# First attention scores asked for three gate tiles later, and the scans' loads in another order

## The chip, the cores and the metric

The kernel runs on one core of a Trainium2 chip. The metric is the device time of one execution in microseconds (us), lower is better. Three runs of the kernel before gave 1560.87, 1555.83 and 1557.04 us: median 1557.04. The engines are named as in the profile: PE (TensorE matmul) with PEld (its weight loads), DVE (VectorE), ACT (ScalarE), POOL (GpSimd), SP (SyncE, which here only issues DMAs).

## What is computed

One layer of a diffusion backbone over 1024 latent tokens and 256 context tokens, width 1024, fp32. Half of the width is a gated DeltaNet with 4 heads of 128, scanned forward and backward, the other half a neighbourhood attention with 8 heads of 64. Cut to the parts that the change touches:

```python
# group A: one scan per direction, chunk by chunk
v_new = u_i - w_i @ S
o_i = (q_i * exp(gam_i)) @ S + qk_i @ v_new
S = S * exp(g_last) + k_dec.T @ v_new
o = rms_norm(o_f + rev(o_b), out_norm_w) * silu(z)      # z: the output gate
# group B: softmax over window keys and all context keys
s = concatenate([q @ k_win + bias, q @ k_ctx])
o = softmax(s) @ v
x = x + g1 * (concatenate([dn_x, na_x]) @ w_out)
x = x + g2 * swiglu(modulate(rms_norm(x)))
```

## The kernel before

The program runs in stages, all unrolled: the modulation and norm; a list of input projections ("jobs"); the two scans with the attention beside them; the output projection; the feed-forward net. A matmul in fp32 precision is made from split operands (a high and a low part), so most products are three matmuls.

**The last projections.** The jobs are column blocks of the combined input projection. The last three are value blocks of the DeltaNet and, as the very last job, `Wide("z", 0)`: half of the gate z. It has eight tiles of 128 tokens (line 595, 24 matmuls of 128x256 each). Beside its tiles run the transposes of the last two value blocks (line 527), which DVE scales (line 531) and SP stores to the DRAM tensor `v_d` (line 535).

**The attention** is a generator, `attention` (called `fill` where it is stepped). Its first step loads heads, context values and the first biases. It has 32 pairs (two heads x one 128-query block). A pair takes two steps' worth of scores (line 303, written S below, one half for each head), a maximum on DVE (305), an exponential on ACT (307), scaling on DVE (308, 309), transposes on PE (314, T below), a copy by ACT (317), and the product with the values (324, PV below). The score banks `sc` have two buffers, the bias tiles `bt` four, so each new pair's biases wait until an older pair is transposed; `bt` is cleared in part by POOL (271) and loaded by SP (272).

**The scans** work through ten chunks of 128 tokens in each direction. `load` issues a chunk's tiles on SP: keys by features `kT`, values `v`, keys by tokens `kt`, queries by features `qT`, the block inverse `y`, and `at`. `scan` uses them in this order: for all but the first chunk `kT` with the state (line 1195); `qT` with the state (1205) from chunk 2 on; `y` with the values (1214); `at` (1226); `kt` for the new state (1231). The first chunk of a direction has no state, so its first matmul is that of `y` and `v`. For every step of a scan or of `finish`, `beside(PACE)` adds PACE to a counter, and each whole unit in it steps the attention once.

**What sets the order.** Program order is only a wish: a list scheduler places each instruction on its engine's queue by priority and by its own reckoning of when operands are ready. On the chip every engine then runs its queue strictly in order, and so does SP with its DMAs: an SP row that has to wait holds all rows behind it.

Of the kernel before, what the change touches and what calls it, by code (L numbers as in the profile page):

```python
# [51 lines left out]
NCONST = 4 * 128 + 4 * 32  # L52
WIN = (256, 0)
CTX = {256: slice(0, 256), 0: slice(384, 640)}
PACE = 0.63
AHEAD = {(1, 0): (3,), (1, 1): (3, 4), (2, 0): (4, 5), (2, 1): (5, 6, 7), (3, 0): (6, 7)}
ORDER = [list(range(NCH)), [1, 0] + list(range(9, 1, -1))]

# [30 lines left out]
def hybrid(ctx, tc, a, dbg):  # L89
# [3 lines left out]
    def pools(stack, name, side=None, bufs=1, **kw):  # L93
        if side:
            kw["side"] = side
        return stack.enter_context(tc.tile_pool(name=name, bufs=bufs, reuse_waits="tile", **kw))
# [43 lines left out]
    v_d = dram.tile([T, 512], F32, name="v_d", tag="v_d")  # L140
    k_d = dram.tile([T, 512], F32, name="k_d", tag="k_d")
    z_d = dram.tile([L, 512], F32, name="z_d", tag="z_d")
    kT_d = dram.tile([128, NCH, 4, 128], F32, name="kT_d", tag="kT_d")
    qT_d = dram.tile([128, 8, 4, 128], F32, name="qT_d", tag="qT_d")
# [6 lines left out]
    y_d = dram.tile([2, NCH, 128, 4, 128], F32, name="y_d", tag="y_d")  # L151
# [102 lines left out]
    def attention(nw):  # L254
# [74 lines left out]

        order = [(hp, half, cb) for hp in range(NAH // 2) for half in range(2) for cb in range(4)]  # L330
        heads = {0: [load(0), load(1)]}
        vcs = {0: context(0)}
        bt, vw = biases(*order[0]), values(*order[0])
        yield 1
        old = None
        for n, (hp, half, cb) in enumerate(order):
            if half == 1 and cb in (0, 2) and hp + 1 < NAH // 2:
                heads.setdefault(hp + 1, []).append(load(2 * hp + 2 + cb // 2))
                if cb == 0:
                    vcs[hp + 1] = context(hp + 1)  # L340
            if cb == 0:
                out = nw.tile([128, 512], F32, name="no", tag="no")
            if old:
                next(old)
            cur = pair(heads[hp], bt, vw, vcs[hp], half, cb, out)
            next(cur)
            if n + 1 < len(order):
                bt, vw = biases(*order[n + 1]), values(*order[n + 1])
            yield 1
            if old:  # L350
                next(old)
                if cb == 0:
                    store(*done)
            if cb == 3:
                done = out, hp, half
            old = cur
            yield 1
# [17 lines left out]
    with ExitStack() as bs:  # L375
# [537 lines left out]
        fl = lambda x: x.rearrange("p a b -> p (a b)")  # L913
# [126 lines left out]
        def blk(n):  # L1040
            return jobs[n] if 0 <= n < len(jobs) and isinstance(jobs[n], Block) else None
# [9 lines left out]
        for n in range(2, len(jobs) + 2):  # L1051
            j = jobs[n] if n < len(jobs) else None
            if n == inv:
                early.close()
                psum.append(psa.enter_context(tc.tile_pool(name="psa", bufs=1, space=PSUM)))
                bg.add(block_inverses())
                bg.add(preps())
            final = n == len(jobs) - 1
            if n == len(jobs) - 2:
                bg.drain()  # L1060
                bg2.drain()
                late.close()
                sp1 = pools(middle, "sp1", "left")
                zpool[0] = sp1
                jobs[n + 1].room()
                fill = attention(pools(attn, "nw", "left", 2))
                next(fill)
            if final:
                psa.close()
                psum.append(scan_psum.enter_context(tc.tile_pool(name="psg", bufs=1, space=PSUM)))  # L1070
            if n + 1 < len(jobs):
                jobs[n + 1].prefetch()
            fin = blk(n - 2) if n - 2 not in done else None
            fin = fin.finish() if fin else iter(())
            nrm = blk(n - 1)
            if isinstance(j, Wide):
                for t, _ in enumerate(j.tiles()):
                    if t > 1 or not final:
                        next(fin, 0)
                    if final:  # L1080
                        next(fill)
                    if t == 4 and nrm:
                        nrm.norm()
                        for _ in fin:
                            pass
                        fin = nrm.finish()
                        done.add(n - 1)
                        nrm = None
                    bg.step(2)
            elif j:  # L1090
                for k in range(KT):
                    j.mm([k])
                    if k >= 3:
                        next(fin, 0)
                    bg.step(1)
                    if n > inv + 4:
                        bg2.step(1)
                j.evac()
            for _ in fin:
                pass  # L1100
            done.add(n - 2)
            if isinstance(j, Wide) and n == values:
                vlat = nv_d[CT:].rearrange("(r c) d -> r c d", c=64)
                for cb in range(4):
                    for ch in range(4):
                        for r in range(4):
                            sp.dma_start(vw_d[r * 32:r * 32 + 32, :, cb, ch],
                                         vlat[4 * ch + r, BLKS[cb]:BLKS[cb] + 32].rearrange("c (h d) -> c h d", d=128))
            if nrm:
                nrm.norm()  # L1110
            if isinstance(j, Block):
                j.silu()
# [7 lines left out]
    fl = lambda x: x.rearrange("p a b -> p (a b)")  # L1120
# [20 lines left out]
    with ExitStack() as gs:  # L1141
# [10 lines left out]
        def work(name, bufs=2, dt=F32):  # L1152
            return sw.tile([128, 4, 128], dt, name=name, tag=name, bufs=bufs)
# [6 lines left out]
        def load(d, c, near):  # L1160

            def tile_of(name, src):
                t = work(name, 3) if name == "v" else sl.tile([128, 4, 128], F32, name=name, tag=name)
                sp.dma_start(fl(t), src)
                return t

            both = shared.pop(c, None)
            if both is None:
                r = slice(c * 128, (c + 1) * 128)
                both = [tile_of("kT", fl(kT_d[:, c])), tile_of("v", v_d[r])]  # L1170
                both += [tile_of("kt", k_d[r]), tile_of("qT", fl(qT_d[:, c - 2])) if c >= 2 else None]
                if c in near:
                    shared[c] = both
            y = tile_of("y", fl(y_d[d, c]))
            at = tile_of("at", fl(at_d[d, c - 2])) if c >= 2 else None
            kT, v, kt, qT = both
            ready[d, c] = kT, qT, kt, v, y, at

        seen = set()
# [102 lines left out]
        def beside(n):  # L1282
            count[0] += n
            while count[0] >= 1:
                count[0] -= 1
                next(fill, 0)

        for d in range(2):
            load(d, ORDER[d][0], (ORDER[1 - d][1],))
        for i in range(NCH):  # L1290
# [5 lines left out]
            while live:  # L1296
                nxt = []
                for n, g in enumerate(live):
                    if next(g, 0):
                        nxt.append(g)  # L1300
                    beside(PACE)
                live = nxt
# [51 lines left out]
    class Stream:  # L1354
# [67 lines left out]
        def next(self, n=2):  # L1422

            while len(self.got) < n:
                self.make()
            out = [self.got.pop(0) for _ in range(n)]
            return out
# [347 lines left out]
```

## Time and profile before

| what | value |
|---|---|
| median of three runs | 1557.04 us (1555.83 to 1560.87) |
| profiled execution, its own time | 1556.61 us |
| its span, first to last instruction | 1554.8 us |
| mean granted TensorE clock | 0.979 |
| last gate tiles, about | 556 to 608 us |
| scans and attention, about | 608 to 820 us |
| output projection and feed-forward net | 820 us to the end |
| DMA traffic | 267.35 MB, mean 172 GB/s |

The span is cut into stages by the lines that run in them. In a row of the windows view stand the stretch, its length, then for each engine the busy time in us with the number of instructions, then the granted TensorE clock, the share of the DMA engines that is busy, and GB/s. In the view of waits a row says which engine and line waited for which engine and line (or DMA): the total in us, how often, and the longest. In the timeline the first two numbers are the start and the duration in us, and a bracket at the end tells the idle time before and what ended it. PE's matmuls are pipelined, so the durations of neighbours overlap; what a group costs is read from its start to the next one's start.

### The profile page before, as it was taken

Reading aid. Unit: us, or ns where it says so; the run is one execution under the profiler, and the core shown is the slowest. Engines: PE = TensorE matmul, PEld = TensorE weight load, DVE = VectorE, ACT = ScalarE, POOL = GpSimd, SP = SyncE. Lnnn points to the kernel's source line nnn. Section 1 sums busy time; section 2 is a strip of 40 time slices with the busy share of each in tenths; the row PEclk is TensorE's granted clock in tenths of the full one; section 3 lists DMA queues with packets and bytes.
Section 4 is the critical chain, followed back from the end, with each engine's and each line's share of the span. In section 5 each row is a group of like instructions: output and inputs, shape, how many; then the busy total and the mean of one; then the engine's idle time right before and its main releaser. Section 6 shows DMA issues by size and latency. Waiting matters only on the chain. (4 is left out here: it accounts for less than half of the span.)

```text
span 1554.8 us, 23965 instructions
## 1 busy us (share of the span) xinstructions
PE 1486.3 (96%) x8702; PEld 1239.4 (80%) x8702; DVE 993.5 (64%) x1712; ACT 727.8 (47%) x1404; POOL 234.1 (15%) x286
## 2 busy tenths in 40 slices
PE   6999999999899978999999999999999999999998
PEld 4788787677678858888887878888888888888887
DVE  5774496674454544667986559865666656689652
ACT  5442552535754336665874266333333334454440
POOL 1154500733625110111210000000000000000000
PEclk9999998899989979999999999999999999999999
DMA  9274221578545466888737601632222224698742
GB/s 388 62 222 126 72 75 55 163 228 241 191 145 183 137 186 193 298 275 265 241 101 246 228 34 59 225 107 105 102 102 102 103 101 156 228 376 290 243 143 82
DMA packets 204118, 267.35 MB, mean 172 GB/s; under 512 B 16736, under 2 KB 114528, under 8 KB 202976
## 3 DMA queue, kind: packets, MB, share of 16 engines
q1 hardware_dynamic: 198480, 261.07, 50.7%
q10 hardware_dynamic: 5520, 4.76, 0.9%
q8 instruction: 68, 1.11, 0.3%
q14 instruction: 50, 0.41, 0.1%
HBM read 201.02 MB, written 68.94 MB: 174 GB/s over the span
## 5 line engine op out<-in xcount | busy, mean ns | idle before, releaser
L405 PE MATMUL blk<-hh,whi 128*128 128x512 f32 (+1 forms) x410 | 124.3, 396 | 2.4 <-ACT kk L550 1.4
L1412 ACT CAST uhi<-wq 128x512 fp32r<-128x512 f32 x101 | 61.0, 622 | 131.9 <-issue 84.9
L1412 ACT CAST uhi<-ws 128x512 fp32r<-128x512 f32 x91 | 54.0, 621 | 146.4 <-PE ps L1351 96.5
L405 PE MATMUL blk<-hl,whi 128*128 128x512 f32 (+1 forms) x410 | 117.5, 379 | 0.3 <-DVE hl L707 0.3
L595 PE MATMUL blk<-zw,hh 128*128 128x256 f32 (+1 forms) x576 | 115.2, 294 | 0.9 <-ACT kk L550 0.8
L405 PE MATMUL blk<-hh,wlo 128*128 128x512 f32 (+1 forms) x410 | 115.1, 378 | 0.6 <-POOL wlo L200 0.6
L1413 DVE TENSOR_TENSOR ulo<-wq,uhi 128x512 fp32r<-128x512 f32 x101 | 67.6, 687 | 58.8 <-ACT uhi L1412 32.4
L1351 PE MATMUL ps<-hT,uhi 128*128 128x512 f32 x336 | 103.6, 390 | 0.0
L1351 PE MATMUL ps<-lT,uhi 128*128 128x512 f32 x336 | 103.5, 389 | 0.0
L1351 PE MATMUL ps<-hT,ulo 128*128 128x512 f32 x336 | 103.5, 389 | 0.0
L595 PEld LDWEIGHTS blk<-zw,hh 128*128 128x128 f32 x576 | 93.0, 193 | 4.7 <-issue 2.0
L1351 PE MATMUL ps<-hB,uhi 128*128 128x512 f32 x288 | 89.2, 391 | 0.6 <-ACT hB L1526 0.6
L1351 PE MATMUL ps<-lB,uhi 128*128 128x512 f32 x288 | 88.8, 389 | 0.4 <-DVE lB L1527 0.4
L1351 PE MATMUL ps<-hB,ulo 128*128 128x512 f32 x288 | 88.7, 389 | 0.0
L405 PEld LDWEIGHTS blk<-hh,wlo 128*128 128x128 f32 x410 | 72.7, 193 | 15.4 <-POOL wlo L200 0.9
L405 PEld LDWEIGHTS blk<-hh,whi 128*128 128x128 f32 x410 | 69.9, 194 | 18.6 <-issue 4.5
L405 PEld LDWEIGHTS blk<-hl,whi 128*128 128x128 f32 x410 | 72.9, 193 | 14.5 <-DVE hl L707 0.8
L595 PE MATMUL blk<-zw,hl 128*128 128x256 f32 (+1 forms) x288 | 83.5, 290 | 0.0
L1351 PEld LDWEIGHTS ps<-hT,ulo 128*128 128x128 f32 x336 | 63.1, 188 | 13.2
L1351 PEld LDWEIGHTS ps<-lT,uhi 128*128 128x128 f32 x336 | 63.1, 188 | 13.1
L1351 PEld LDWEIGHTS ps<-hT,uhi 128*128 128x128 f32 x336 | 62.9, 188 | 12.9
L200 POOL TENSOR_TENSOR wlo<-wraw,whi 128x1024 fp32r<-128x1024 f32 x18 | 45.3, 2517 | 180.6 <-ACT whi L199 173.2
(359 smaller groups left out, 3544.5 us busy)
## 6 DMA issues: line engine op xcount, KB each, us to landing
wq<-w_fo SPq DMA_DIRECT2D x99, 256.0 KB, 4.3
wq<-w_gu SPq DMA_DIRECT2D x88, 256.0 KB, 2.8
wad<-wa SPq DMA_DIRECT2D x64, 256.0 KB, 4.6
bt<-rpb SPq DMA_DIRECT2D x64, 192.0 KB, 3.5
t_d<-g SPq DMA_DIRECT2D x22, 512.0 KB, 3.6
fr<-t_d SPq DMA_DIRECT2D x44, 256.0 KB, 5.1
f_d<-g SPq DMA_DIRECT2D x33, 256.0 KB, 2.1
fr<-f_d SPq DMA_DIRECT2D x33, 256.0 KB, 4.1
```

The costliest lines, as they stand in the source:

```text
L200: lo_engine.tensor_tensor(o, r, h.bitcast(F32), OP.subtract)
L405: pe.matmul(o, ww[:, k], xx[k][:, s], start=k == 0 and j == 0, stop=k == KT - 1 and j == 2)
L595: pe.matmul(p[:, :c1 - c0], x[k][:, s], ww[:, k, c0:c1], start=k == 0 and j == 0, stop=k == KT - 1 and j == 2)
L1351: pe.matmul(o, w[wi][:, k], x[xi][:, k], start=first and k == 0 and j == 0, stop=k == n - 1 and j == 2, skip_group_check=True)
L1412: act.copy(hi, self.raw[key])
L1413: dve.tensor_tensor(lo, self.raw[key], hi.bitcast(F32), OP.subtract)
```

## The change

Three edits. In the last gate job the attention is stepped only from the fourth tile on, so five times and not eight. PACE goes from 0.63 to 0.66. In the scans' `load` the order of the issues in the program is `v`, `kt`, `y`, `kT`, `qT`, `at`, where it was `kT`, `v`, `kt`, `qT`, `y`, `at`. No operation is added or removed.

```diff
-PACE = 0.63
+PACE = 0.66
...
                 for t, _ in enumerate(j.tiles()):
                     if t > 1 or not final:
                         next(fin, 0)
-                    if final:
+                    if final and t > 2:
                         next(fill)
...
             if both is None:
                 r = slice(c * 128, (c + 1) * 128)
-                both = [tile_of("kT", fl(kT_d[:, c])), tile_of("v", v_d[r])]
-                both += [tile_of("kt", k_d[r]), tile_of("qT", fl(qT_d[:, c - 2])) if c >= 2 else None]
+                both = [tile_of("v", v_d[r]), tile_of("kt", k_d[r])]
+                y = tile_of("y", fl(y_d[d, c]))
+                both += [tile_of("kT", fl(kT_d[:, c])), tile_of("qT", fl(qT_d[:, c - 2])) if c >= 2 else None]
                 if c in near:
                     shared[c] = both
-            y = tile_of("y", fl(y_d[d, c]))
+            else:
+                y = tile_of("y", fl(y_d[d, c]))
             at = tile_of("at", fl(at_d[d, c - 2])) if c >= 2 else None
-            kT, v, kt, qT = both
+            v, kt, kT, qT = both
             ready[d, c] = kT, qT, kt, v, y, at
```

The lines behind the edit in `load` move down by two (1214 becomes 1216, 1231 becomes 1233). What the scheduler makes of it is seen on the engines' queues, at three places. Rows are instructions in queue order; names carry a number for each buffer.

**PE, where the last projection block (405) meets the attention and the gate.** `sc_5126` and `sc_5233` are the scores of pairs 0 and 1, `blk` a gate tile. The changed kernel has:

```order
L405 MATMUL blk_4894<-hh7_458,wlo_4711 128x512
L303 MATMUL sc_5126<-kh_4859,qs_4858 128x256
L303 MATMUL sc_5233<-kh_4859,qs_4858 128x256
L303 MATMUL sc_5126<-kh_4867,qs_4866 128x384
L314 MATMUL sc_5126<-cst_72,bt_4876 128x128 x2
L595 MATMUL blk_5005<-zw_4854,hh0_129 128x256
```

Here nothing moved. Row for row the kernel before has the same lines and forms in the same places, down to the end of the third gate tile: the scheduler puts the scores of the first pairs ahead of the gate in both. Only the numbers of two score buffers differ.

**PE, from the last gate tile to the scans' first matmul.** One row stands for each group (its first row). Before, with `sc_5252`, `sc_5371`, `sc_5555`, `sc_5630` the scores of pairs 2, 3, 4, 5:

```order
L595 MATMUL blk_5399<-zw_4854,hh7_458 128x256
L527 MATMUL m_5427<-cst_72,cacc_4985 128x128 x2
L324 MATMUL sc_5252<-pt_5362,vc_4874 64x128
L314 MATMUL sc_5371<-cst_72,bt_5272 128x128 x5
L303 MATMUL sc_5555<-kh_4859,qs_4858 128x256
L314 MATMUL sc_5371<-cst_72,bt_5275 128x128 x5
L324 MATMUL sc_5371<-pt_5546,vc_4874 64x128
L314 MATMUL sc_5555<-cst_72,bt_5391 128x128 x5
L303 MATMUL sc_5630<-kh_4859,qs_4858 128x256
L1214 MATMUL ps_5509<-v_5490,y_5494 128x128 x4
```

Now, with `sc_5233`, `sc_5350`, `sc_5511` the scores of pairs 1, 2, 3:

```order
L595 MATMUL blk_5304<-zw_4854,hh7_458 128x256
L527 MATMUL m_5332<-cst_72,cacc_4985 128x128 x2
L314 MATMUL sc_5233<-cst_72,bt_5146 128x128 x5
L303 MATMUL sc_5350<-kh_4859,qs_4858 128x256
L314 MATMUL sc_5233<-cst_72,bt_5149 128x128 x5
L324 MATMUL sc_5233<-pt_5341,vc_4874 64x128
L314 MATMUL sc_5350<-cst_72,bt_5253 128x128 x5
L303 MATMUL sc_5511<-kh_4859,qs_4858 128x256
L314 MATMUL sc_5350<-cst_72,bt_5256 128x128 x4
L1216 MATMUL ps_5445<-v_5424,y_5428 128x128 x4
```

The scans' first matmul follows the gate after nearly the same amount of attention, but that attention is two pairs younger: the groups between the gate tiles went behind the gate.

**SP, from the loads of the first output weights (195) to the scans' first `y`.** In brackets stand the semaphores a row waits for; a DMAHW one is an earlier DMA's landing. Before:

```order
L195 DMA wraw<-w_out 128x8x128 [waits DMAHW2_49,PE_49]
L195 DMA wraw<-w_out 128x8x128 [waits DMAHW3_49]
L535 DMA v_d<-vt 128x10x128 [waits DMAHW4_49,DVE_49]
L272 DMA bt<-rpb 128x384 [waits DMAHW5_49,DMAHW6_49,PE_49,Pool_49]
L278 DMA vw<-vw_d 128x384 [waits DMAHW7_49]
L272 DMA bt<-rpb 128x384 [waits DMAHW0_49,PE_49,Pool_49]
L1164 DMA kT<-kT_d 128x512 [waits DMAHW1_49]
L1164 DMA v<-v_d 128x512 [waits DMAHW4_49,DMAHW2_49]
L1164 DMA kt<-k_d 128x512 [waits DMAHW3_49,Activation_49]
L1164 DMA y<-y_d 128x512
```

Now:

```order
L195 DMA wraw<-w_out 128x8x128 [waits DMAHW5_49,PE_49]
L195 DMA wraw<-w_out 128x8x128 [waits DMAHW6_49]
L272 DMA bt<-rpb 128x384 [waits DMAHW7_49,PE_49,Pool_49]
L535 DMA v_d<-vt 128x10x128 [waits DMAHW0_49,DVE_49]
L272 DMA bt<-rpb 128x384 [waits DMAHW2_49,PE_49,Pool_49]
L1164 DMA v<-v_d 128x512 [waits DMAHW3_49,DMAHW0_49]
L1164 DMA kt<-k_d 128x512 [waits DMAHW4_49]
L1164 DMA y<-y_d 128x512 [waits DMAHW5_49,Activation_49]
```

`v` now leads the scans' loads, `y` is third and not fourth, and a bias load stands ahead of the last value store. In both, the first `v` waits for that store's landing. From the output projection (line 1328 before) to the end PE's queue is the same in both kernels.

## Prediction

> **What bounds the kernel now.** I read the page first, then the windows by stage, PE's waits, and the timelines of PE and SP where the windows showed idle time. The page's first part and two of its slice rows:
>
> ```profile
> PE 1486.3 (96%) x8702; PEld 1239.4 (80%) x8702; DVE 993.5 (64%) x1712; ACT 727.8 (47%) x1404; POOL 234.1 (15%) x286
> ...
> PE   6999999999899978999999999999999999999998
> PEclk9999998899989979999999999999999999999999
> ```
>
> PE is busy for 96% of the span, the next engine, DVE, for 64%. Only slices 14 to 16 of 40 (39 us each, 544 to 622 us) show PE with a visible hole, and the clock row dips there too. By stage (stretch, length, busy us of PE, PEld, DVE, ACT, POOL, then clock, DMA share, GB/s):
>
> ```profile
> 556.40:570.90 14.50, 3.98 (x18) 2.20 (x19) 10.50 (x17) 5.59 (x8) 0.77 (x3) 0.57 1.07 291
> 570.90:607.60 36.70, 36.56 (x306) 34.54 (x304) 13.51 (x31) 16.49 (x33) 3.97 (x7) 0.94 0.43 124
> 607.60:626.00 18.40, 13.72 (x108) 11.05 (x106) 9.08 (x20) 14.81 (x29) 2.51 (x5) 0.81 0.99 327
> 626.00:820.00 194.00, 190.18 (x1793) 167.05 (x1792) 150.70 (x456) 134.18 (x383) 30.19 (x61) 1.00 0.73 233
> ...
> 835.00:1554.80 719.80, 714.58 (x3162) 590.47 (x3160) 469.16 (x738) 287.89 (x486) 0.00 (x0) 1.00 0.46 158
> ```
>
> The first row is the opening, between the last value block and the gate: PE does 4.0 us of work in 14.5, at a clock of 0.57. The second is the gate, full. The third is the seam between the gate and the scans: 13.7 of 18.4 busy, clock 0.81. In the fourth, scans and attention, PE is idle for 3.8 us of 194; in the rest of the kernel it is full. So a change here gains by closing the opening or the seam, and in the fourth stage it can gain 3.8 us at most. PE's waits in the opening:
>
> ```profile
> PE sc L303 <- DMA kh<-nk_d: 4.9, 1, 4.9
> PE sc L303 <- DVE mx L305: 3.6, 1, 3.6
> PE sc L314 <- DVE bt L309: 1.9, 1, 1.9
> ```
>
> Together 10.4 us: the first scores wait for the keys' landing, then for the maximum on DVE, then the first transposes for the scaled exponentials.
>
> **The opening: nothing.** The edit asks for the first scores three tiles later, but PE's queue has them where they were, ahead of the gate, row for row to the third gate tile. SP's, ACT's, DVE's and POOL's queues are the same up to there too. The 10.4 us stay. The edit does not do here what it says.
>
> **The seam.** What moves is the attention between the gate tiles. From the order rows, these groups went from before to behind the gate's end: T and PV of pair 1, S and T of pair 2, S of pair 3. Their price stands where scan and attention alternate without a wait (start to next start):
>
> ```profile
> 631.87 0.76 PE L314 MATMUL sc<-cst,bt 128*128 128x128 f32 x5
> 632.47 0.61 PE L1214 MATMUL ps<-vn,y 128*128 128x128 f32 x4
> 632.92 0.27 PE L303 MATMUL sc<-kh,qs 128*128 128x256 f16 x1
> ...
> 633.46 1.28 PE L1214 MATMUL ps<-vn,y 128*128 128x128 f32 x10
> 634.67 0.32 PE L324 MATMUL sc<-pt,vc 128*64 128x128 f32 x1
> ...
> 635.91 0.33 PE L314 MATMUL sc<-cst,bt 128*128 128x128 f32 x1
> ```
>
> Half a T takes 632.47 - 631.87 = 0.60, half an S 633.46 - 632.92 = 0.54, a PV 635.91 - 634.67 = 1.24. A pair is 2 x 0.60 + 2 x 0.54 + 1.24 = 3.5 us. What moved is two T, two S and a PV: 2.4 + 2.2 + 1.2 = 5.8 us. Now the seam's clockwork before:
>
> ```profile
> 607.35 0.38 PE L527 MATMUL m<-cst,cacc 128*128 128x128 f32 x2
> ...
> 620.73 1.13 PE L1214 MATMUL ps<-v,y 128*128 128x128 f32 x8 [1.33 <-DMA y<-y_d]
> ...
> 625.03 1.06 PE L1231 MATMUL ps<-vk,kt 128*128 128x128 f32 x8
> ...
> 626.02 0.32 PE L324 MATMUL sc<-pt,vw 128*64 128x128 f32 x1
> ```
>
> ```profile
> 605.99 1.30 SPq L195 DMA_DIRECT2D wraw<-w_out  x2
> 608.22 0.49 SPq L535 DMA_DIRECT2D v_d<-vt  x1
> ...
> 613.95 0.33 SPq L272 DMA_DIRECT2D bt<-rpb  x1
> 614.33 0.43 SPq L1164 DMA_DIRECT2D kT<-kT_d  x1
> 614.86 0.38 SPq L1164 DMA_DIRECT2D v<-v_d  x1
> ...
> 615.76 0.63 SPq L1164 DMA_DIRECT2D y<-y_d  x1
> ```
>
> The gate ends at 607.35, where the last transposes (527) start. The values are stored at 608.22, the scans' first `v` is issued at 614.86, `y` at 615.76, and the scans' first matmul runs at 620.73 after 1.33 us of waiting for `y`. From 626.02 on PE is full. How long the transfers took from issue to landing (the last value store, the one before it, the scans' first `y`, and all 20 `y` by their median):
>
> ```profile
> v_d<-vt SPq DMA_DIRECT2D x1, 640.0 KB, 6.5
> ...
> v_d<-vt SPq DMA_DIRECT2D x1, 640.0 KB, 4.2
> ...
> y<-y_d SPq DMA_DIRECT2D x1, 256.0 KB, 4.8
> ...
> y<-y_d SPq DMA_DIRECT2D x20, 256.0 KB, 4.0
> ```
>
> The store of 608.22 landed after 6.5 us, at 614.7, and `v`, which waits for it, was issued 0.1 later: this store gates the scans, not the order of the loads behind it.
>
> The same chain in the changed kernel, from the gate's new end at 607.35 - 5.80 = 601.55. A bias load now stands ahead of the store. It waits for half a T of pair 1 and for POOL's clearing of the tile:
>
> ```profile
> 614.00 0.31 POOL L271 MEMSET bt<- 128x256 f32 x1 [3.90 <-DVE mx L308]
> ```
>
> So: 601.55 + 0.3 (527) + 0.60 (T) + 0.31 (POOL) + 0.33 (an issue, as the row at 613.95) = 603.1 for the store; without that row it would be 602.4. Landing: 4.2 us if it goes as the store before it, 6.5 if as the last one. The two output weights that compete with it are issued 1.36 us ahead of the gate's end (605.99) and so lead the store by 2.9 us and not 2.2; I take 5.8. `v` follows 0.1 later, `y` 0.90 after `v` (`kt` stands between them in the old order and in the new; what the new order saves is `kT` in front, 0.5 us, and that stood in the shadow of the store). `y` lands in 4.0 to 4.8. The first scan matmul, 0.2 after that: 603.1 + 5.8 + 0.1 + 0.9 + 4.8 + 0.2 = 614.9, with 612.5 and 615.6 as the ends. That is 5.8 us earlier than 620.73, with 7.0 us more attention still to do: at 626.02, where the scans' first steps are done and PE is full, pairs 0 to 3 were finished before; at the same place in the new queue pairs 0 and 1 are. Break-even is therefore 626.0 - 7.0 = 619.0 for that place.
>
> By the Trainium skill, "DMA: Bandwidth & Descriptors", section "Anatomy of one DMA — SWDGE (gpsimd) path", a transfer costs about 2.0 us plus its bytes at 436 GB/s; an estimate for this store's 655,360 bytes is 3.5 us. The trace does not agree: 6.5 and 4.2 for the same store, and the fit is of another issuing path. By 3.5 the first scan matmul would come at 612.6, and the sum would be 2.3 us lower, 0.4 faster than before.
>
> From the first scan matmul to that place took 626.02 - 620.73 = 5.3 us before; the second direction's `y` still comes four issues after the first's, so 5.3 stays. On top comes the clock. Between 601.6 and the first scan matmul PE has about 5.4 us of work for 13.3 us, and its last 4 to 5 us are one wait, since T of pair 2 (its last row) is ahead of the scan in the queue and everything else behind it. After the opening's wait the clock went like this, with PE at work again from 570.6:
>
> ```profile
> 570.00:575.00 5.00, 4.25 (x19) 3.80 (x20) 3.98 (x7) 2.95 (x6) 2.62 (x2) 0.50 0.50 161
> 575.00:580.00 5.00, 5.00 (x42) 5.00 (x42) 0.00 (x0) 0.70 (x2) 0.00 (x0) 0.96 1.00 268
> ```
>
> Half speed up to about 575.3, 4.7 us into the work. The 5.3 us hold 3.6 us of work; at half speed for 4.7 us some of it fits the wait for the second `y`. Cost: 0 if it all fits, 1.5 at most, I take 0.7. Sum: 614.9 + 5.3 + 0.7 = 620.9 against 619.0, **1.9 us slower**. Early ends: 612.5 + 5.3 = 617.8, 1.2 faster. Late ends: 615.6 + 5.3 + 1.5 = 622.4, 3.4 slower.
>
> **PACE and the rest.** `beside` is called 6 + 9 x 8 + 3 x 6 = 96 times. Before, 1 + 8 steps are used up and 58 calls of the attention remain; 58 / 0.63 = 92.1. Now 1 + 5 are, and 61 / 0.66 = 92.4. Both run out on the 93rd call, and the queues agree from the last pair's transposes on. The attention per unit of scan work is 5% denser, but PE is the full engine there, so time stretches with it and DVE's and ACT's share stays. Taken as 0 beyond the 7.0 us already counted; the bounds are the two rivals. The loads' new order in this stage (`y` ahead of `kT` and `qT`) costs nothing while each lands a chunk ahead; no PE wait there named a DMA before.
>
> **Forecast, 0.55: no change that can be told.** The sum is made on the profiled execution: 1556.6 + 1.9 = 1558.5. The median of the runs is 0.4 above that execution, so 1558.9 for a median. Its own range, with 2 us for the fourth stage, is 1554 to 1562.
>
> **Rival, slower, 0.30: biases late behind `y`.** SP's queue is strict. `y` needs its slot back from the matmul of an earlier chunk, and now it stands ahead of `kT`, `qT`, and of biases that the scheduler put behind it. Before:
>
> ```profile
> SPq L1164 <- PE ps L1214: 6.8, 8, 2.7
> ...
> DVE bt L305 <- DMA bt<-rpb: 1.3, 1, 1.3
> ...
> bt<-rpb SPq DMA_DIRECT2D x64, 192.0 KB, 3.5
> ```
>
> SP's scan loads waited 8 times for that slot, 0.85 us in the mean, 2.7 at worst; biases held DVE up once, for 1.3. If each of nine chunks holds the queue for 2.7 and not 0.85, SP falls 1.85 us behind per chunk. The bias tiles are filled a pair ahead and cover more than half; at 0.7 us of PE per chunk it is 9 x 0.7 = 6.3 more, 1558.9 + 6.3 = 1565. It decides as soon as a bias is issued later than one landing (3.5 us) before its pair's maximum. Against it: that one bias wait is all there was in the stage.
>
> **Rival, faster, 0.15: early landing and a smoother mix.** The store lands in 4.2, `y` in 4.0, the clock costs nothing (1.2 faster), and the denser attention fills the 3.8 us of idle time in the fourth stage: 1557.0 - 5.0 = 1552. For it: DMA is lighter at the gate (0.43) than in the seam (0.99). Against it: 3.8 is already thin, and its waits are ends of chains.
>
> **Numbers.** About 0.3% (4.7 us) is what a measurement of this kernel can tell from no change. The forecast puts 0.50 within that and 0.05 above; the slower rival 0.30 above; the faster one 0.03 within and 0.12 below. Range: from the faster rival to just past the slower one, 1552 to 1566.
>
> **What would show it.** The opening row again at 4 of 14.5 busy with the same three waits: right about the queue. Gate end near 601.6, store near 603, first scan matmul near 615 with a single wait of 4 us or more for `y` or `v`, then half the clock for a few us: right about the seam. If the first scan matmul comes before 611 the store did not gate. If waits of PE on line 314 or of DVE on biases add up to over 4 us between 620 and 820, the slower rival holds. An opening shorter by over 3 us would overturn the argument.

## The result, and the profile after

The changed kernel took 1557.85 us (median of 20 runs, 1546.13 to 1563.32), the kernel before 1558.06 us in the same series (20 runs, 1553.12 to 1561.20): ratio 0.9994, 95% interval 0.9979 to 1.0009. No difference that can be told. The page of the changed kernel, engines and two slice rows:

```profile
PE 1483.4 (95%) x8702; PEld 1237.6 (80%) x8702; DVE 989.5 (64%) x1712; ACT 727.7 (47%) x1404; POOL 235.4 (15%) x286
...
PE   6999999999899977999999999999999999999999
PEclk9999998899999988999999999999999999999999
```

The hole is where it was, in slices 14 to 16. The windows over the same stretches as before, opening, gate, seam, scans:

```profile
556.40:570.90 14.50, 5.16 (x23) 3.43 (x24) 10.60 (x18) 5.92 (x10) 1.42 (x1) 0.59 1.04 287
570.90:607.60 36.70, 33.21 (x281) 30.55 (x279) 8.99 (x19) 15.39 (x26) 2.13 (x5) 0.98 0.53 153
607.60:626.00 18.40, 13.91 (x94) 12.09 (x95) 7.79 (x18) 10.29 (x29) 0.94 (x3) 0.72 0.81 281
626.00:820.00 194.00, 190.45 (x1807) 167.70 (x1807) 152.03 (x468) 138.09 (x378) 32.47 (x65) 1.00 0.74 231
```

The opening is as thin as before (the 1.2 us more are gate tiles, since this execution arrived there 0.9 us earlier). The seam is still 13.9 of 18.4 busy, and the gate's row now has a hole of its own at its end. PE's timeline of the changed kernel, first the opening, then the seam:

```profile
560.03 0.58 PE L303 MATMUL sc<-kh,qs 128*128 128x256 f16 x2 [4.59 <-DMA kh<-nk_d]
...
566.24 0.37 PE L303 MATMUL sc<-kh,qs 128*128 128x256 f16 x1 [3.77 <-DVE mx L305]
...
569.40 0.66 PE L314 MATMUL sc<-cst,bt 128*128 128x128 f32 x2 [1.94 <-DVE bt L309]
569.71 0.56 PE L595 MATMUL blk<-zw,hh 128*128 128x256 f32 x1
...
600.04 0.38 PE L527 MATMUL m<-cst,cacc 128*128 128x128 f32 x2
...
614.25 2.05 PE L1216 MATMUL ps<-v,y 128*128 128x128 f32 x8 [3.46 <-DMA y<-y_d]
...
620.71 0.32 PE L324 MATMUL sc<-pt,vc 128*64 128x128 f32 x1
```

The same three waits stand in the opening, 10.3 us (before 10.4), ahead of the first gate matmul. The gate ends 7.3 us earlier than at 607.35, the first scan matmul comes 6.5 us earlier than at 620.73 (line 1214 before is 1216 now; 0.9 us of both is this execution's earlier arrival), and ahead of it stands one wait of 3.46 us. Why it is there shows SP's queue in the seam, then SP's waits, then the landing times of the two transfers:

```profile
601.03 0.36 SPq L272 DMA_DIRECT2D bt<-rpb  x1
601.49 0.39 SPq L535 DMA_DIRECT2D v_d<-vt  x1
604.45 0.50 SPq L272 DMA_DIRECT2D bt<-rpb  x1
609.70 0.32 SPq L1164 DMA_DIRECT2D v<-v_d  x1
...
610.59 0.38 SPq L1164 DMA_DIRECT2D y<-y_d  x1
```

```profile
SPq L1164 <- DMA v_d<-vt: 4.7, 1, 4.7
```

```profile
v_d<-vt SPq DMA_DIRECT2D x1, 640.0 KB, 8.2
...
y<-y_d SPq DMA_DIRECT2D x1, 256.0 KB, 3.5
```

The values are stored at 601.49, and SP stands for 4.7 us until that store has landed; only then are the scans' first loads issued. So the seam did not get shorter (14.1 us from the gate's last matmul to the first scan matmul, 13.2 before), and what the gate gave, 6.1 us, comes back behind the first scan matmul, where the scans' stretch is 7.6 us longer (table below).

### The profile page after: what moved, and what is told of

Read it like the earlier page. It is cut to its first block, busy times and chain, and to the rows that moved or that the text cites. A ratio compares the mean times of both kernels' runs of the same rounds, so it can differ in the third digit from the quotient of the medians.

```text
span 1555.5 us, 23971 instructions
## 1 busy us (share of the span) xinstructions
PE 1483.4 (95%) x8702; PEld 1237.6 (80%) x8702; DVE 989.5 (64%) x1712; ACT 727.7 (47%) x1404; POOL 235.4 (15%) x286
## 3 DMA queue, kind: packets, MB, share of 16 engines
q8 instruction: 68, 1.11, 0.3%
## 5 line engine op out<-in xcount | busy, mean ns | idle before, releaser
L405 PEld LDWEIGHTS blk<-hl,whi 128*128 128x128 f32 x410 | 72.9, 193 | 14.5 <-DVE hl L707 0.8
L1353 PEld LDWEIGHTS ps<-lT,uhi 128*128 128x128 f32 x336 | 63.1, 188 | 13.2
L1353 PEld LDWEIGHTS ps<-hT,ulo 128*128 128x128 f32 x336 | 63.1, 188 | 13.1
```

The lines of the kernel that those rows point to most:

```text
L405: pe.matmul(o, ww[:, k], xx[k][:, s], start=k == 0 and j == 0, stop=k == KT - 1 and j == 2)
L1353: pe.matmul(o, w[wi][:, k], x[xi][:, k], start=first and k == 0 and j == 0, stop=k == n - 1 and j == 2, skip_group_check=True)
```

## The experiments

Executions reach the opening at different times (549.7 to 559.0 us in the profiles below), so places are counted inside the stage. From PE's timeline of each run: **opening**, from the end of the value blocks' last matmul (line 405) to the first gate matmul (595); **gate**, to the end of the last 595; **seam**, to the first scan matmul (`ps<-v,y`); **scans**, to the first matmul of the output projection. "First load" is how far behind the last 595 SP issues the scans' first load. All in us.

| run | opening | gate | seam | scans | sum | first load |
|---|---|---|---|---|---|---|
| before | 14.6 | 36.6 | 13.2 | 200.0 | 264.4 | 6.8 |
| before, again (e12) | 14.6 | 36.6 | 13.1 | 201.2 | 265.4 | 6.8 |
| changed | 14.3 | 30.5 | 14.1 | 207.6 | 266.4 | 9.5 |
| changed, again (e11) | 14.9 | 31.7 | 12.4 | 205.7 | 264.7 | 7.0 |
| e1, later scores alone | 14.7 | 30.5 | 12.7 | 207.4 | 265.4 | 4.6 (`v` 8.0) |
| e2, loads' order alone | 15.0 | 37.1 | 12.6 | 202.9 | 267.6 | 6.5 |
| e3, changed, values from keys | 14.8 | 30.5 | 11.4 | 205.6 | 262.3 | 4.6 |
| e4, changed, weights first | 4.3 | 35.1 | 13.7 | 207.4 | 260.4 | 8.6 |
| e5, changed, values early | 14.7 | 31.3 | 10.3 | 205.5 | 261.8 | 4.7 |
| e6, changed, both edits | 4.4 | 35.1 | 10.2 | 206.0 | 255.6 | 4.6 |
| e7, before, both edits | 4.0 | 42.3 | 13.3 | 200.2 | 259.8 | 7.0 |
| e8, changed, move doubled | 14.5 | 29.2 | 12.8 | 213.9 | 270.3 | 8.5 |
| e9, e7 and loads' order | 3.9 | 41.8 | 11.7 | 201.3 | 258.6 | 6.5 |
| e10, e7 and later scores | 4.1 | 35.2 | 10.7 | 204.9 | 255.0 | 4.6 |

The two pairs of unchanged kernels tell how much of this is scatter: up to 1.7 us in the sum. (The 13.8 us that some expectations below give for the changed kernel's seam count from the end of the last transposes, line 527; from the gate's last matmul it is 14.1.)

**e1 and e2: each part alone.**

```diff
-PACE = 0.63
+PACE = 0.66
-                    if final:
+                    if final and t > 2:
```

> The change's first part alone: the first scores three gate tiles later and the pace of 0.66, with the scans' loads in their old order. Theory (moved attention is zero-sum, and the last value store's landing sets the seam): opening 556.4 to 570.9 us keeps about 4 of 14.5 us busy on PE with its waits for the keys and the masked maxima, the gate still ends near 600 us instead of 607.35, the first scan matmul comes at 614 to 617 us, and the total is 1558 within 3 us. Rival 1 (the two parts cancel, and this one costs): keys by features ahead of values and the inverse make the first scan matmul come after 618 us, and the total is 3 to 6 us above before. Rival 2 (this part gains and the loads' order loses): 3 us or more below before.

Measured: 1558.63 us, before 1558.13, ratio 1.0002 (0.9988 to 1.0016). As the theory has it: the opening untouched, the gate 6.1 us shorter, the scans 7.4 longer. (The gate's end, forecast near 600, was 604.3, because this execution came to the opening 3.5 us later than that of the changed kernel.)

```diff
-                both = [tile_of("kT", fl(kT_d[:, c])), tile_of("v", v_d[r])]
+                both = [tile_of("v", v_d[r]), tile_of("kt", k_d[r])]
...
```

> The change's second part alone: the new order of the scans' loads (values, keys by tokens, inverse, then keys and queries by features), with the attention and the pace as before. Theory: the first load of the scans is now the one that waits for the last value block's store, and every later load stands behind it in SP's queue, so keys by features lose their head start; the first scan matmul stays within 1.5 us of the 620.7 us of before, and the total within 2 us of it. Rival (the order of loads is what the first scan waits for): values and the inverse land about 2 us earlier, the first scan matmul comes at 618 to 619 us, and the total is 2 us or more below before.

Measured: 1558.02 us, ratio 1.0004 (0.9984 to 1.0025). This execution came to the opening 4.8 us early, so the absolute place of the first scan matmul says nothing; behind the gate it is 12.6 us, 13.2 before. The total is the theory's, its reason is not quite: here SP did not wait for the store at all, though by little: the store left at 604.35 and took 5.5 us, and `v` was issued at 610.09. The largest of its waits in e2 between 585 and 620 us is for PE's transposes, ahead of bias loads, and none names the store:

```profile
SPq L272 <- PE sc L314: 7.8, 6, 3.6
```

So in the old order of the attention a second thing holds the scans' loads back, the biases of pairs that are not yet transposed.

**e3: no load waits for the store.** The scans' values are read from the stored keys instead.

```diff
-                both = [tile_of("v", v_d[r]), tile_of("kt", k_d[r])]
+                both = [tile_of("v", k_d[r]), tile_of("kt", k_d[r])]
```

> The changed kernel, with the scans' values read from the stored keys by tokens instead of from the stored values: the result is another one, the number, size and shape of the loads is the same, and no load of the scans waits any longer for the last value block's store. Theory (the store's landing of 8.2 us gates the scans): the 4.7 us wait of SP's queue for the store is gone, the scans' first load issues 3 to 8 us earlier than 609.7 us, PE's wait of 3.5 us for the inverse shrinks under 1 us, the clock does not fall to half at 610 to 620 us, and the total is 3 to 6 us below that of the changed kernel. Rival 1 (something behind it is due at nearly the same time: the inverse's own store, or the queue's bias loads): the first load moves less than 1.5 us, and the total is the same within 1.5 us. Rival 2 (the seam's time comes back in the fourth stage, because work is only moved ahead): the first scan matmul comes 4 us or more earlier, and the total still is the same within 1.5 us.

Measured: 1553.46 us, ratio 0.9977 (0.9963 to 0.9992). SP's queue in the seam, and PE's wait for the inverse:

```profile
603.01 0.39 SPq L535 DMA_DIRECT2D v_d<-vt  x1
605.99 0.33 SPq L272 DMA_DIRECT2D bt<-rpb  x1
606.38 1.14 SPq L1164 DMA_DIRECT2D v<-k_d  x1
```

```profile
PE ps L1216 <- DMA y<-y_d: 1.9, 2, 1.1
```

The first load follows the last bias at once, 4.6 us behind the gate, the clock stays full through the seam, and 4.4 us come out at the end (PE's longest wait for the inverse is 1.1 us, just over the 1 us expected). The store's landing gates the seam of the changed kernel.

**e4: the gate's weights first.** The last gate's weights are asked for before the attention's first loads and not behind them; ACT and POOL split them. It is the second half that moves: SP issues it at 556.99, where before it was issued at 563.61, behind the loads of the heads.

```diff
                 fill = attention(pools(attn, "nw", "left", 2))
+                jobs[n + 1].prefetch()
                 next(fill)
...
-            if n + 1 < len(jobs):
+            if n + 1 < len(jobs) and n != len(jobs) - 2:
```

> The changed kernel, with the loads of the last gate's second weight half issued ahead of the attention's first loads, so that the gate's tiles can stand ahead of the first scores in PE's queue. Theory (the opening is lost because the queue keeps the first scores ahead of the gate, whose weights come late): the gate's first matmul comes at 561 to 566 us instead of 569.7, PE's waits between 556 and 571 us fall from 10.3 to 3 to 6 us, the gate ends 3 to 7 us earlier plus what scores leave its front, and the total is 4 to 8 us below that of the changed kernel. Rival 1 (the gate's weights are not ready any earlier, since their conversion on POOL and DVE is what is late): the opening's waits stay at 9 us or more, and the total within 2 us. Rival 2 (the scores moved out come back as idle time at the seam, where the store's landing is waited for): the opening gains 4 us or more, the wait ahead of the first scan matmul grows by the same, and the total stays within 2 us.

Measured: 1552.03 us, ratio 0.9964 (0.9945 to 0.9983), 5.8 us below the changed kernel. The opening in e4:

```profile
563.18 0.58 PE L595 MATMUL blk<-zw,hh 128*128 128x256 f32 x1 [4.26 <-ACT zw L587]
...
566.43 0.80 PE L595 MATMUL blk<-zw,hh 128*128 128x256 f32 x2 [2.03 <-POOL zw L588]
```

Now the gate opens and the first scores follow behind its fourth tile, which is what the change asked for. Two waits for the split of the weights remain, 6.3 us (a little over the 3 to 6 expected); the three waits of the attention, 10.3 us, are covered by gate tiles. Opening and gate together fall from 44.8 to 39.3 us, and the seam does not take it back.

**e5: the last values earlier.** Norm and transposes of the last value block at the third gate tile instead of the fifth.

```diff
-                    if t == 4 and nrm:
+                    if t == (2 if final else 4) and nrm:
```

> The changed kernel, with the norm and the transposes of the last value block at the last gate's third tile instead of its fifth, so that the store of the values leaves SP some tiles before the gate ends. Theory (the store's landing gates the scans, and nothing else is due before it): the store issues at least 5 us before the gate's last matmul, SP's queue no longer waits for it, the first scan matmul comes 10.5 to 11.5 us behind the gate's end as without that wait in the values-from-keys run (13.8 in the changed kernel), and the total is 3 to 5 us below the changed kernel, 1553 to 1555 us. Rival 1 (the scans' loads stay where the bias loads and the scheduler's queue put them): first scan matmul still 13 to 14 us behind the gate's end, total within 1.5 us of 1558. Rival 2 (the norm's vector work delays the attention's maxima or the gate's own steps): PE stands still inside the gate by 2 us or more, and the total is 1558 or above.

Measured: 1553.31 us, ratio 0.9982 (0.9963 to 1.0001). SP's queue of e5:

```profile
594.71 0.37 SPq L535 DMA_DIRECT2D v_d<-vt  x1
...
601.91 3.98 SPq L272 DMA_DIRECT2D bt<-rpb  x2
605.99 0.40 SPq L1164 DMA_DIRECT2D v<-v_d  x1
```

The store is out 6.6 us before the gate's end, the first load comes 4.7 us behind it, as in e3 by another way, and the seam is 10.3 us (11.4 in e3). The interval only touches 1; that the gain is real rests on the profile and on e6.

**e6 and e7: both edits, on the changed kernel and on the kernel before.**

> The changed kernel with both edits: the last gate's second weight half loaded ahead of the attention's first loads, and the last value block's norm at the third tile. Theory (the opening's waits and the store's landing are two separate losses of about 6 and 4 us): the gate's first matmul some 4 us behind the value blocks' last one as in the weights-first run (14 to 15 us before), the first scan matmul within 12 us of the gate's end, and a total of 1547 to 1549.5 us, 8.5 to 11 us below before. Rival (the two share one limit: with the gate earlier, the inverse's loads and the bias loads are late instead): no more than 1.5 us below the weights-first run, that is 1550.5 us or above.

Measured: 1548.34 us, ratio 0.9934 (0.9910 to 0.9959), 9.4 us below the kernel before. The two losses are separate: 5.8 and 4.5 us alone, 9.5 together, against the changed kernel's median (the kernel before had 1558.06, 1558.13 and 1557.72 in the three series, so they can be set side by side).

> Both edits on the kernel before, so without the change's later scores, pace and load order. Theory (the change itself is zero-sum; what the later scores need is a gate whose weights are there): the gate starts after about one tile's worth of matmuls, the first scores' waits for the maxima are filled by gate tiles, and the total is within 2 us of the run of both edits on the changed kernel. Rival (the later scores pay once the weights come first, since scores, maxima and biases need the gate's first tiles as cover): 2.5 us or more above that run.

Measured: 1553.81 us, ratio 0.9971 (0.9953 to 0.9990): 5.5 us above e6. The theory fell and the rival's number came true: once both holders are out of the way, the change is worth something. The rival's reason is not what the profile shows, since in e7 too the first scores' waits are filled by gate tiles, but for 0.9 us. What differs is the seam. SP in the seam, e7 first, then e6 (the scans' first load is the last row of each):

```profile
598.58 4.91 SPq L272 DMA_DIRECT2D bt<-rpb  x2
603.54 0.43 SPq L1165 DMA_DIRECT2D kT<-kT_d  x1
```

```profile
597.21 3.96 SPq L272 DMA_DIRECT2D bt<-rpb  x2
601.23 0.60 SPq L1165 DMA_DIRECT2D v<-v_d  x1
```

The gate's last matmul ends at 596.56 in e7 and at 596.59 in e6. In e7 the attention is further on, SP waits 7.9 us for PE's transposes before it may fill bias tiles (3.9 in e6), and the scans' first load leaves 2.3 us later (603.54 - 601.23). The seam is 3.1 us longer for it, most of the 4.2 us between the two sums.

**e9 and e10: which part makes the 5.5 us.** e7 with the loads' new order alone, and with the later scores and their pace alone.

> The two edits of the both run on the kernel before, with the change's order of the scans' loads alone: attention from the first gate tile, pace 0.63. The run of both edits on the changed kernel was 1548.3 us, that on the kernel before 1553.8 us; this one and the next tell which part of the change makes the 5.5 us between them. Theory (the later scores make it: without them a further pair's bias loads stand in SP's queue ahead of the scans' first load and wait for PE): the seam from the gate's last matmul to the first scan matmul stays at 12.5 to 13.5 us, and the total at 1552 to 1555 us. Rival (the order of loads makes it, since the store no longer holds the values back): seam of 10 to 11 us, total 1548 to 1550 us.

> The two edits of the both run on the kernel before, with the change's later scores and pace of 0.66 alone, the scans' loads in the old order. Theory (the later scores make the 5.5 us): seam of 10 to 11.5 us, total 1548 to 1550.5 us. Rival (the order of loads makes it): seam of 12.5 us or more, total 1552 to 1555 us.

Measured: e9 1553.21 us, ratio 0.9959 (0.9936 to 0.9982); e10 1547.46 us, ratio 0.9921 (0.9893 to 0.9948). The later scores make it. The two intervals overlap a little, but the sums of the stage say the same, 258.6 and 255.0, and e10 is at e6's level without the new order. e9's seam, 11.7 us, lies between the two forecasts, so the order of loads may be worth a microsecond there; no total shows it. The seam is also only 0.9 of the 3.6 us between the sums of e9 and e10; the rest is a gate that is 6.6 us shorter against scans that are only 3.6 us longer. Part of that may be the clock, which was at half speed for 3.4 us of e9's scans and not in those of e10, e6 and e7; how the gain splits is not settled. e10 and e6 are the best kernels of this study, and they differ by less than their intervals.

**e8: the move doubled.**

```diff
-PACE = 0.66
+PACE = 0.69
-                    if final and t > 2:
+                    if final and t > 5:
```

> The changed kernel with the move doubled: the attention starts to be drawn after six gate tiles instead of three, with a pace of 0.69. Theory (moved attention is zero-sum): the opening of the stage still stands still for about 10 us, the gate ends another 4 to 7 us earlier than 45 us behind the value blocks' last matmul, the first scan matmul follows 12 to 14 us behind its end, and the total is 1557 to 1561 us. Rival 1 (more attention behind the gate covers the wait for the store and the inverse): total 3 us or more below 1558. Rival 2 (attention is needed beside the scans only up to a point, and what is left runs bare at the end of the scans): the fourth stage's output projection starts 3 us or more later than 266.4 us behind the value blocks' last matmul, total above 1561 us.

Measured: 1564.00 us, ratio 1.0044 (1.0027 to 1.0061). The theory missed: the gate became only 1.3 us shorter, since little attention was left beside it, and the scans 6.3 us longer. By the windows view, PE is busy for 206.5 us of the scans' stretch (203.5 in the changed kernel's first execution), 3.0 us more, and idle for 3.3 us more; where the added work comes from stays open. Rival 2's two numbers came true (sum 3.9 us up, total above 1561), though not bare at the end: the idle time is spread. Ahead of the first scan matmul PE waits longer than in any other profile here:

```profile
614.84 2.05 PE L1216 MATMUL ps<-v,y 128*128 128x128 f32 x8 [4.67 <-DMA y<-y_d]
```

**e11 and e12: the same two kernels once more.**

> The changed kernel once more, unchanged, for a second profiled execution: how far the seam's terms vary from one execution to the next. In the first one the last value block's store took 8.2 us to land, the inverse's first load 3.5 us, the first scan matmul came 13.8 us behind the gate's last matmul, and the output projection 266.4 us behind the value blocks' last one. If 8.2 us is what the store takes in this kernel, it is 7.5 us or more again; if it was the traffic of one execution, it lies between 5.3 and 7.5 us, and the place of the output projection within 1.5 us of the first.

> The kernel before once more, unchanged, for a second profiled execution. In the first one the first scan matmul came 13.2 us behind the gate's last matmul and the output projection 264.4 us behind the value blocks' last one, 2.0 us less than in the changed kernel, while the medians of the two are equal within 0.3 us. If the 2.0 us belong to the kernels, this execution shows 263.5 to 265.5 us; if they belong to the executions, it shows 265.5 us or more.

The single times were 1555.71 (changed) and 1558.17 us (before). SP's queue in the changed kernel's second execution, and the landings of the store and of the first `y`:

```profile
602.70 0.34 SPq L272 DMA_DIRECT2D bt<-rpb  x1
603.14 0.39 SPq L535 DMA_DIRECT2D v_d<-vt  x1
606.12 0.33 SPq L272 DMA_DIRECT2D bt<-rpb  x1
608.85 0.32 SPq L1164 DMA_DIRECT2D v<-v_d  x1
```

```profile
v_d<-vt SPq DMA_DIRECT2D x1, 640.0 KB, 5.7
...
y<-y_d SPq DMA_DIRECT2D x1, 256.0 KB, 4.4
```

The store took 5.7 us this time, so 8.2 was that one execution; the output projection's place differs by 1.7 us from the first, a little more than the 1.5 expected. The sums went the other way too: 264.7 for the changed kernel, 265.4 for the one before. By its own number e12 still fits "belongs to the kernels"; with e11 beside it, the difference of 2.0 us in the first pair is scatter.

## Why the prediction held, step by step

**The opening: nothing changes.** Right. The same three waits, 10.3 us for 10.4, in the same place. e4 adds what the prediction left unsaid: the first scores stood ahead because the gate's second weight half was asked for behind the attention's loads, so the gate could not open first. With the weights ahead, the scheduler's queue does move the scores.

**The seam's places.** Forecast and the two executions, by the prediction's landmarks: gate's end (the start of line 527) 601.55 (600.04 and 601.71), store 603.1 (601.49 and 603.14), first scan matmul 614.9 (614.25 and 614.28). Both executions came to the opening about 1 us earlier than the profile that the sum starts from (0.9 and 1.1 us); inside the stage the first scan matmul is at 615.1 and 615.3. The terms in between were mis-sized for the first execution: the landing, taken as 5.8 with 6.5 as its upper bound, was 8.2, and `y`, taken as 4.8 with 4.0 as its lower bound, was 3.5; the two errors of +2.4 and -1.3 and the earlier store cancelled, which was luck. In the second execution both terms lay within their bounds, 5.7 and 4.4. The bounds came from two landings of one execution, which was too few: over all runs here the last store landed in 3.7 to 8.2 us.

**The wait and the clock at the seam.** The single wait of 4 us or more ahead of the first scan matmul, named as a sign, did not come: it was 3.46 us, and 1.11 us in the second execution, where half the clock (606.7 to 613.5) fell on the attention ahead of it and filled the time. Two rows of the second execution, the scans' first matmul and the place up to which the sum was made:

```profile
614.28 1.13 PE L1216 MATMUL ps<-v,y 128*128 128x128 f32 x8 [1.11 <-DMA y<-y_d]
...
619.11 0.32 PE L324 MATMUL sc<-pt,vc 128*64 128x128 f32 x1
```

Between them lie 4.83 us, in the first execution 6.46 (614.25 to 620.71) and before 5.3. So the clock's price behind the first scan matmul, taken as 0.7, was 1.2 with half speed lying there and nothing when it was over by then. In the scans' stretch PE was busy for 203.5 and 200.8 us in these two executions of one kernel; the forecast could not know which.

**"This store gates the scans".** Right for the changed kernel (e3, e5). For the kernel before it was half of the truth: the bias load issued at 613.95 and the store's landing at 614.7 were ready within 1 us of each other. Of SP's waits before the change, between 600 and 620 us, the largest entry is for PE's transposes, ahead of bias loads, and none names the store:

```profile
SPq L272 <- PE sc L314: 6.8, 4, 3.7
```

And e2 and e7 show that the biases alone hold the first load 6.5 to 7.0 us behind the gate. This is why the change gains nothing at the seam: the later scores take the biases out of the way, which would be worth 2.3 us at the first load (e7 and e6), and the store, asked for after the gate's last tiles, keeps the loads where they were.

**The attention's price.** 7.0 us behind the first scans were forecast; the scans' stretch grew by 7.6 us in the first pair of executions and by 4.5 in the second. The gate gave 6.1 and 4.9. So the move is zero-sum here, and the **1.9 us slower** of the sum (first pair +2.0, second -0.7) is below what these runs can tell.

**Loads' order: nothing.** Right: e2 alone, and e10 against e6.

**PACE and the fourth stage: 0.** PE is busy for 190.45 of 194 us, 190.18 before. The slower rival's signs are there, in SP's and DVE's waits of the changed kernel in that stage:

```profile
SPq L1164 <- PE ps L1216: 11.5, 11, 2.7
```

```profile
DVE bt L305 <- DMA bt<-rpb: 3.3, 1, 3.3
```

Before, these were 6.8 and 1.3. With PE's own waits on line 314 between 620 and 820 us, 0.9 in all and no more than before, the 3.3 make 4.2 us, just over the 4 us that were to show that the slower rival holds. PE did not pay for it all the same, so that sign was badly chosen: a wait of DVE need not reach PE. Nor does e8, where more of the same costs 6 us, bear the rival's mechanism out: DVE waits there for a bias load for 0.6 us in all, and PE's idle time in the scans is made of small waits, most of them for ACT and DVE.

## What to carry to other kernels

Where several things hold one queue back, moving one of them shows nothing until the others are gone: the same edit was worth nothing that shows here and 5.5 us with the store and the weights out of the way. For a strict DMA queue, write down for the load that matters how far behind the last work ahead of it it is issued, and try each holder by taking it away alone; a load that reads back what the kernel has just stored pays the store's landing, so let that store go several tiles earlier. And take a second execution before reading 2 us out of a profile.

## What the runs showed of the hardware

**The clock goes by stretches of 3.4 us.** Before the change no gap in the seam was over 1.33 us, and still the clock fell to half. Its two switches lie at 612.9 and 619.7; cut at these points, the seam of the kernel before:

```profile
609.50:612.90 3.40, 1.56 (x14) 1.10 (x12) 0.83 (x2) 3.08 (x5) 0.31 (x1) 1.00 1.12 326
612.90:616.30 3.40, 2.62 (x22) 2.22 (x22) 2.27 (x6) 3.14 (x6) 0.31 (x1) 0.50 1.00 332
616.30:619.70 3.40, 3.10 (x19) 2.20 (x15) 1.39 (x2) 2.39 (x5) 1.08 (x2) 0.50 0.97 342
619.70:623.10 3.40, 2.22 (x17) 1.82 (x17) 2.45 (x6) 2.12 (x7) 0.80 (x2) 0.99 0.96 360
```

Half speed lasted 6.8 us here, in e4, in e11 and in e12, 10.2 us in the changed kernel's first execution and 3.4 us in e1: once, twice or three times 3.4. In the clock's record of each of the fourteen profiles all switches lie on such a grid. Cut on it, the stretches of the seams after which the clock fell held at most 1.57 us of PE work, those after which it stayed full at least 1.59; it came back after 2.95 us or more and not after 2.76 or less. So within these seams scattered gaps count together, the limit lies near half of a stretch, and the price depends on where the stretches happen to lie: the changed kernel's seam cost 10.2 us at half speed once and 6.8 the next time. This is no rule for the whole kernel. Earlier in the kernel before, the clock fell behind a stretch in which PE was busy throughout, with 16 matmuls of one column (line 486) among its rows:

```profile
298.90:302.30 3.40, 3.40 (x33) 2.83 (x32) 0.46 (x2) 1.61 (x5) 2.87 (x11) 1.00 0.27 99
302.30:305.70 3.40, 3.40 (x27) 2.49 (x26) 0.42 (x1) 1.14 (x4) 0.02 (x1) 0.50 0.00 0
```

What counts is therefore not the profile's busy time alone, and what else it is stays open. The Trainium skill, "TensorE: Matmul & The Clock Gate", section "What's actually happening", has a free-running window of 3413 ns, half speed after an idle window and full after a busy one. The grid agrees with these runs; the windows that led to half speed in these seams were not idle, with up to 1.57 us of work in them.

**The same 640 KB store took 3.7 to 8.2 us to land.** It took 3.7 to 4.1 when it left in the middle of the gate (e5, e6, e7, e9, e10), with 182 to 221 GB/s of DMA traffic in all while it was under way, and 5.5 to 8.2 at the gate's end, with 271 to 348 GB/s. What makes 8.2 of 5.7 in the same kernel stays open; the slower one had less traffic beside it, 271 against 338 GB/s.
